# Linear attention's second product on whole 128x128 blocks instead of 64x64 and 128x64 pieces

## The chip, the cores and the metric

The kernel runs on one core of a Trainium2 chip. A core has a matrix engine (TensorE, PE in the profile; its weight loads are PEld), a vector engine (VectorE, DVE), a scalar engine (ScalarE, ACT), GpSimd (POOL) and SyncE (SP), which here issues the transfers. Each engine works through its own list of instructions in order; semaphores hold it until what it needs is there. The metric is the device time in microseconds (us) of one execution. Lower is better. Three runs of the kernel before gave 322.04, 321.97 and 322.44 us.

## The reference

One decoder layer on 256 tokens of width 1024, in fp32. An input projection feeds two groups of heads: MoBA, which is plain causal attention here, and GLA, a gated linear attention with 4 heads, keys of width 64 and values of width 128. Then come an output projection, a residual and a feed-forward part with a short convolution. The change is in GLA:

```python
def gla_attention(q, k, v, log_a):
    """S_t = diag(alpha_t) S_{t-1} + k_t^T v_t ;  o_t = q_t S_t."""
    ...
        decay = jnp.exp(jnp.where(causal[None, None, :, :, None], diff, -jnp.inf))
        A = jnp.einsum('bhtd,bhsd,bhtsd->bhts', q_, k_, decay)
        o = (jnp.einsum('bhts,bhsv->bhtv', A, v_)
             + jnp.einsum('bhtd,bhdv->bhtv', q_ * jnp.exp(G_), state))
```

Written without chunks, `o[t] = sum over s <= t of A[t, s] v[s]`, where `A[t, s]` is the product of query t and key s with the decay between them. `A` is causal: nothing stands where s is after t. Behind it, `o` is normed per head, multiplied by a gain and by the gate `silu(r)`.

## The kernel before

The 256 tokens are two token tiles of 128 (`tt` = 0, 1). Weights come in slots of 1 MB; ScalarE and VectorE split each into a high part `hi` (line 92) and a rest `lo` (line 95), and `mm3` multiplies in three products (lines 109 to 111). TensorE's list is in the order of the program text. The input projection and the first half of the output projection run in steps `q` = 0 to 55, and a table (`on(q, f, ...)`) says behind which step each piece of attention is put. The lists of ScalarE, VectorE, GpSimd and SyncE are ordered by the compiler's scheduler, except where the text fixes them (`g_tail`).

GLA first builds `A` transposed: rows are s, columns are t. There are 8 diagonal blocks of 128x128, one for each of 2 head pairs, 2 token tiles and 2 heads in a pair. A block has four quadrants of 64. The two on the diagonal, (s, t) both in the first half or both in the second, are collected in `ATd`: seven levels of halving (`lvl_a` to `lvl_d_`) write into it, on VectorE (line 376). The quadrant with s in the first half and t in the second comes from the level of 64, which `lvl_d_` copies from PSUM on ScalarE into rows 0 to 63 of `ATu` (line 371). `lvl_join` (line 379) copies the second diagonal quadrant below it, into rows 64 to 127 of `ATu`. The fourth quadrant, s in the second half and t in the first, is zero and is stored nowhere. `AT01` holds the blocks between the two token tiles, for the 4 heads (line 403).

`g_av(tt)` is the second product, `o = A v`, for one token tile, with the blocks as TensorE's stationary operand (weights) and the values `gv` as the moving one. For each head, with `o` a 128x128 part of one PSUM bank:

```python
if tt == 1:
    T.matmul(o, AT01[:, pr * 2 + hh], gv[:, 0, vs], start=True, stop=False)
i = (pr * 2 + tt) * 2 + hh
T.matmul(o[0:64], ATd[0:64, i], gv[0:64, tt, vs], start=(tt == 0), stop=True)
T.matmul(o[64:128], ATu[:, i], gv[:, tt, vs], start=(tt == 0), stop=True)
```

Lines 420 and 421 are the two pieces: tokens of the first half from 64 rows and 64 columns, tokens of the second half from 128 rows and 64 columns. Line 418 is a whole block. Both token tiles are put behind step 46, and two steps of the input projection and the last MoBA product (lines 526 and 527) stand between them and the output projection. Then `g_tail` norms both tiles on ScalarE and VectorE (lines 429, 177, 178, 435), loads the gate's table and evaluates the gate (line 409). `g_out` multiplies by the gate (line 450) and transposes (line 452), behind steps 53 and 54; its result is a part of the output projection's input.

Of the kernel before, what the change touches and what calls it, by code (L numbers as in the profile page):

```python
# [9 lines left out]
F32 = mybir.dt.float32  # L10
# [6 lines left out]
S = 256  # L17
KT = 8
# [9 lines left out]
LEVELS = [32, 16, 8, 4, 2, 1, 64]  # L28
# columns of the parameter array
P_FG, P_BG, P_CW, P_CB = 0, 8, 10, 10 + 3 * 2 * NP  # L30
# [4 lines left out]
def trunk_kernel(ctx: ExitStack, tc: tile.TileContext, xT_d, wG_d, w5_d, wo_d, up_d, dn_d,  # L35
# [16 lines left out]

    # ------------------------------------------------------------------ constants and parameters
    A.preload_act_table_set("natural_log_exp_and_others")
# [12 lines left out]

    # the tensor engine's clock rises while the first loads are under way
    warm = const.tile([128, 128], F32, name="warm")
# [4 lines left out]

    # ------------------------------------------------------------------ weights: load and split
    RAW, SPL = 4, 3
# [59 lines left out]

    # ------------------------------------------------------------------ x
    xg = main.tile([128, KT + KT * S], F32, name="xg")     # the first norm's gains, then x^T
    pag = xg[:, :KT]
# [33 lines left out]
    def rsqrt_t(r, ss, n, tmp):  # L173
        """r = (ss / n + EPS) ** -0.5 by logarithm and exponential, then a Newton step."""
        v, t = tmp
        V.tensor_scalar(v, ss, 1.0 / n, EPS, op0=ALU.mult, op1=ALU.add)
        A.activation(t, ss, AF.Ln, scale=1.0 / n, bias=eps)
        A.activation(r, t, AF.Exp, scale=-0.5)
        V.tensor_mul(t, r, r)
        V.scalar_tensor_tensor(t, t, -0.5, v, op0=ALU.mult, op1=ALU.mult)  # L180
        V.scalar_tensor_tensor(r, t, 1.5, r, op0=ALU.add, op1=ALU.mult)

    def rsqrt(r, ss, n, tmp):
        """r = (ss / n + EPS) ** -0.5: a seed from the exponent bits, then Newton steps. It yields
        between its steps, so that other work fits in."""
        v, t = tmp
        V.tensor_scalar(v, ss, 1.0 / n, EPS, op0=ALU.mult, op1=ALU.add)
        V.tensor_scalar(t.bitcast(I32), v.bitcast(I32), 1, None, op0=ALU.logical_shift_right)
        yield
        V.tensor_scalar(r.bitcast(I32), t.bitcast(I32), -1.0, float(0x5F3759DF),  # L190
                        op0=ALU.mult, op1=ALU.add)
        for _ in range(3):
            V.tensor_mul(t, r, r)
            yield
            V.scalar_tensor_tensor(t, t, -0.5, v, op0=ALU.mult, op1=ALU.mult)
            V.scalar_tensor_tensor(r, t, 1.5, r, op0=ALU.add, op1=ALU.mult)

    # ------------------------------------------------------------------ attention buffers
    ap_ = ctx.enter_context(ExitStack())
# [4 lines left out]
    Gc = at.tile([128, 512], F32, name="Gc")  # L204
    ATd = at.tile([128, 8, 64], F32, name="ATd")           # the blocks of 64 on the diagonal
    ATu = at.tile([128, 8, 64], F32, name="ATu")           # the second half's columns
    AT01 = at.tile([128, 4, 128], F32, name="AT01")
# [7 lines left out]
    for i in range(2):  # L215
        nc.gpsimd.memset(kts[i], 0.0)
        nc.gpsimd.memset(qts[i], 0.0)
    nc.gpsimd.memset(qt128, 0.0)
    mqT = at.tile([128, 4, S], F32, name="mqT")
    mkT = at.tile([128, 4, S], F32, name="mkT")  # L220
# [30 lines left out]
    def xrow():  # L251
        """The rotation's tables take up the norm, which lies along their rows here."""
        p = att()
        for tt in range(2):
            T.matmul(p[:, tt * 128:(tt + 1) * 128], rstd(tt).to_broadcast([128, 128]), ident,
                     start=True, stop=True)
        for t in (cos, sin):
            V.tensor_mul(t, t, p[:, :S])

    # ---- GLA  # L260
    def g_evac(tt):
# [19 lines left out]
    def g_diag():  # L281
        dgp = at.tile([128, 2, 256], F32, name="e", bufs=2)
        V.scalar_tensor_tensor(dgp, gqk[:, :, 0:256], DK ** -0.5, gqk[:, :, 272:528],
                               op0=ALU.mult, op1=ALU.mult)
        V.tensor_add(id64, ident[:, 0:64], ident[:, 64:128])
        dg = at.tile([128, 2, 2, 2], F32, name="dg")       # pair, ttile, head
        for tt in range(2):
            V.tensor_reduce(dg[:, :, tt, :], dgp[:, tt].rearrange("p (a h d) -> p a h d", a=2, h=2),
                            axis=mybir.AxisListType.X, op=ALU.add)
        for i in range(8):  # L290
            A.activation(ATd[:, i], id64, AF.Copy, scale=dg.rearrange("p a b c -> p (a b c)")[:, i:i + 1])
# [75 lines left out]
    def lvl_d_(l):  # L367
        b = LEVELS[l]
        p = st["lv", l]
        if b == 64:  # L370
            A.activation(ATu[0:64], p[0:64].rearrange("p (i t) -> p i t", i=8), AF.Copy)
            return
        n = 32 // b
        o = ATd.rearrange("p i (n two b) -> p i n two b", two=2, b=b)[:, :, :, 1, :]
        m = lvl[:, l].bitcast(I32).rearrange("p (n b) -> p n b", b=b)[:, None].to_broadcast([128, 8, n, b])
        V.copy_predicated(o, m, p[:, :256].rearrange("p (i n b) -> p i n b", i=8, b=b))  # L376

    def lvl_join():
        A.activation(ATu[64:128], ATd[64:128], AF.Copy)

# [30 lines left out]
    def g_av(tt):  # L411
        p = att()
        for h in range(HG):
            pr, hh = divmod(h, 2)
            o = p[:, h * DV:(h + 1) * DV]
            vs = slice(h * DV, (h + 1) * DV)
            if tt == 1:
                T.matmul(o, AT01[:, pr * 2 + hh], gv[:, 0, vs], start=True, stop=False)
            i = (pr * 2 + tt) * 2 + hh
            T.matmul(o[0:64], ATd[0:64, i], gv[0:64, tt, vs], start=(tt == 0), stop=True)  # L420
            T.matmul(o[64:128], ATu[:, i], gv[:, tt, vs], start=(tt == 0), stop=True)  # L421
        st["o", tt] = p
# [16 lines left out]
    def g_tail():  # L439
        # the norm's tables before the gate's: one change of tables  # L440
        with tc.manual_schedule(engines={mybir.EngineType.Activation}):
# [16 lines left out]

    # ---- MoBA (the sequence is one block, so a query's own block is all it attends to)
    def rope_a(which, n):  # L460
        """The halves of each head change places."""
        qs = at.tile([128, 512], F32, name="qs", bufs=2)
# [16 lines left out]
    def m_scores(pr):  # L479
        # two heads in turn, each in its half of the array's rows and in a bank of its own  # L480
        for hh in range(2):
# [50 lines left out]

    # ------------------------------------------------------------------ emission plan
    plan = {}
# [107 lines left out]

    # ------------------------------------------------------------------ output projection
    hh_ = main.tile([128, KT, S], F32R, name="hh", tag="ah")
# [33 lines left out]

    # ------------------------------------------------------------------ feed-forward
    downs = {}  # L680
# [91 lines left out]

    # the output's columns by bank; the last ones, which end the kernel, are fewer
    PIECES = (((0, 512), (512, 1024)), ((0, 512), (512, 768), (768, 1024)))
# [10 lines left out]
    def residual(tt, n):  # L785
        """The residual opens the down projection's sums."""
        a, b = PIECES[tt][n]
# [22 lines left out]

    # pair 0: its last contraction tile waits for the last columns of h
    up_alloc(0)
# [11 lines left out]
    lo(2, 1)  # L824
    # pair 1
    dload(1)
# [7 lines left out]
    for n, _ in enumerate(steps):  # L834
        if n < 4:
            ups[3].split_lo(512 * n, 512 * n + 512)
    # pair 2
    dload(2)
# [17 lines left out]
    gate_lo(0)  # L856
    # pair 3
    dload(3)
# [63 lines left out]
    A.preload_act_table_set("sqrt_and_others")  # L922
    # the last pair's gate is awaited behind one product of the second token tile
    for i in range(NP - 4, NP - 1):
# [10 lines left out]

    # ------------------------------------------------------------------ final norm
    fin = ff.tile([128, 24], F32, name="fin")
    yy = ff.tile([128, 2, D], F32, name="yy", tag="big")
    for tt in range(2):
# [4 lines left out]
        for n, (a, b) in enumerate(PIECES[tt]):  # L944
# [11 lines left out]
            if n < last:  # L956
                vb = v
                V.tensor_scalar(vh, v, -0.5, None, op0=ALU.mult)
        # r = (mean square + EPS) ** -0.5 with one Newton step
        A.activation(sq, ss, AF.Sqrt, scale=1.0 / D, bias=vb)  # L960
# [10 lines left out]
def _layout(inputs):  # L971
# [5 lines left out]
    def ktile(m):  # L977
        return m.reshape(-1, 128, m.shape[1]).transpose(1, 0, 2)      # [128, k, cols]

# [14 lines left out]
    fin_g = f(np.broadcast_to(a["final_norm_g"].reshape(1, D), (128, D)))  # L994
    # tables that depend on shapes alone
    inv = (1.0 / (np.float32(10000.0) ** (np.arange(0, HD, 2, dtype=np.float32) / np.float32(HD)))).astype(np.float32)
# [32 lines left out]
```

## Time and profile before

| | before |
|---|---|
| median of three runs | 322.04 us (321.97 to 322.44) |
| span of the profiled execution | 320.4 us |
| the time around that span, to the median | 1.6 us |
| mean granted TensorE clock | 0.994 |
| `g_av` in the profile | 92.46 to 99.90 us |
| products in `g_av` | 8 of 64 rows and 64 columns, 8 of 128 rows and 64 columns, 4 whole |

The profile is of one execution. Times in it count from the start of its span; the span leaves out about 1.6 us of what the runs' time includes. A row of the view in order of time gives start, duration, engine, line, operation, output<-inputs, size of the array used (rows*columns, for TensorE), shapes and count; behind it in brackets stands how long the engine was idle before, and what ended that. TensorE's rows overlap, since its products are pipelined, so that the distance of two starts says what an instruction takes of the stream. Every fp32 product is recorded twice (two passes, each with a weight load); the `hi`/`lo` products are recorded once.

### The profile page before, as it was taken

What the parts mean: (1) busy time and instruction counts of PE and PEld (TensorE: products, weight loads), DVE (VectorE), ACT (ScalarE), POOL (GpSimd) and SP (SyncE); (2) the same over time, 40 slices, a digit from 0 to 9 for tenths busy, and PEclk for the clock granted to TensorE, in tenths of its full rate; (3) what the DMA queues carried; (4) which work ended last, traced back from release to release, by engine and by line L of the source; (5) the groups of instructions that cost most, each with busy time, mean ns of one, the idle gap of its engine ahead of it and who ended that gap; (6) DMA issues with size and microseconds to landing.
All of it is one profiled execution on the core that took longest, in us unless ns stands there. A gap on an engine that the chain in (4) does not pass through costs nothing.

```text
span 320.4 us, 5873 instructions
## 1 busy us (share of the span) xinstructions
PE 312.3 (97%) x2312; PEld 285.9 (89%) x2312; DVE 253.7 (79%) x478; ACT 203.2 (63%) x369; POOL 3.5 (1%) x16
## 2 busy tenths in 40 slices
PE   8999999999999999999999999999999999999992
PEld 7999997776766999999999999999999999999982
DVE  3888999999634658899999987777787777776653
ACT  5978988588845748637677655555555555544353
POOL 4000000000000000000000000000000000000000
PEclk9999999999999999999999999999999999999997
DMA  6999433452360245379356555555555521110003
GB/s 186 387 415 402 183 133 131 139 186 79 125 262 1 103 163 190 140 282 370 127 212 254 202 196 196 199 196 198 197 196 199 218 111 68 65 67 1 2 0 132
DMA packets 12299, 55.39 MB, mean 173 GB/s; under 512 B 1376, under 2 KB 2928, under 8 KB 7920
## 3 DMA queue, kind: packets, MB, share of 16 engines
q1 hardware_dynamic: 12272, 55.02, 46.2%
q8 instruction: 18, 0.29, 0.4%
q14 instruction: 9, 0.07, 0.1%
HBM read 53.97 MB, written 1.05 MB: 172 GB/s over the span
## 4 chain that ended last, share of the span: by engine, by line
PE 79%; DVE 9%; ACT 5%; issue 2%; DMA 2%; SPq 1%; DVEq 0%; ACTq 0%
PE att L110 14%; PE att L109 14%; PE att L111 14%; PE acc L110 10%; PE acc L109 10%; PE acc L111 10%; DVE lo L95 2%; DMA xg<-in_xT 2%; ACT qs L465 1%; DVE qt L350 1%; DVE att L494 1%; PE att L421 1%; PE att L420 1%; PE att L526 1%; DVE ATd L376 1%
## 5 line engine op out<-in xcount | busy, mean ns | idle before, releaser
L92 ACT ACTIVATE hi<-raw 128x1024 fp32r<-128x1024 f32 (+3 forms) x84 | 80.1, 971 | 51.4 <-PE att L110 43.1
L95 DVE TENSOR_TENSOR lo<-raw,hi 128x1024 fp32r<-128x1024 f32 (+3 forms) x86 | 93.7, 1098 | 13.8 <-ACT hi L92 13.8
L109 PE MATMUL att<-hh,hi 128*128 128x256 f32 x352 | 98.6, 280 | 0.0
L111 PE MATMUL att<-hh,lo 128*128 128x256 f32 x352 | 98.4, 280 | 0.0
L110 PE MATMUL att<-hl,hi 128*128 128x256 f32 x352 | 98.4, 279 | 0.0
L109 PEld LDWEIGHTS att<-hh,hi 128*128 128x128 f32 x352 | 66.3, 188 | 0.0
L111 PEld LDWEIGHTS att<-hh,lo 128*128 128x128 f32 x352 | 66.2, 188 | 0.0
L110 PEld LDWEIGHTS att<-hl,hi 128*128 128x128 f32 x352 | 66.2, 188 | 0.0
L756 DVE SCALAR_TENSOR_TENSOR c<-us,par,c 128x256 f32<-128x256 f32 x88 | 40.7, 482 | 4.1 <-ACT c L748 2.5
L748 ACT ACTIVATE c<-us,par 128x256 f32<-128x256 f32 x44 | 24.0, 590 | 21.6 <-DVE us L738 16.1
L111 PE MATMUL acc<-dhi,gl 128*128 128x512 f32 (+1 forms) x88 | 32.3, 367 | 0.0
L110 PE MATMUL acc<-dlo,gh 128*128 128x512 f32 (+1 forms) x88 | 32.2, 366 | 0.0
L109 PE MATMUL acc<-dhi,gh 128*128 128x512 f32 (+1 forms) x88 | 31.8, 361 | 0.0
L695 DVE TENSOR_TENSOR dlo<-draw,dhi 128x1024 fp32r<-128x1024 f32 x22 | 26.7, 1220 | 0.0
L738 DVE TENSOR_TENSOR us<-att,rb 128x512 f32<-128x512 f32 x20 | 13.8, 690 | 15.9 <-PE att L111 15.9
L109 PE MATMUL acc<-hi,ah 128*128 128x512 f32 (+1 forms) x64 | 25.9, 404 | 0.2 <-ACT hi L92 0.2
L110 PE MATMUL acc<-lo,ah 128*128 128x512 f32 (+1 forms) x64 | 24.6, 384 | 0.4 <-DVE lo L95 0.4
L111 PE MATMUL acc<-hi,al 128*128 128x512 f32 (+1 forms) x64 | 24.1, 376 | 0.0
L690 ACT ACTIVATE dhi<-draw 128x1024 fp32r<-128x1024 f32 x22 | 23.1, 1048 | 0.0
L110 PEld LDWEIGHTS acc<-dlo,gh 128*128 128x128 f32 x88 | 16.5, 188 | 3.0
L109 PEld LDWEIGHTS acc<-dhi,gh 128*128 128x128 f32 x88 | 16.6, 188 | 2.9
L111 PEld LDWEIGHTS acc<-dhi,gl 128*128 128x128 f32 x88 | 16.5, 188 | 2.6
(192 smaller groups left out, 537.5 us busy)
## 6 DMA issues: line engine op xcount, KB each, us to landing
raw<-in_up SPq DMA_DIRECT2D x22, 1024.0 KB, 4.8
draw<-in_dn SPq DMA_DIRECT2D x22, 512.0 KB, 5.7
raw<-in_w SPq DMA_DIRECT2D x8, 1024.0 KB, 7.4
raw<-in_wo SPq DMA_DIRECT2D x4, 1024.0 KB, 4.7
raw<-in_w SPq DMA_DIRECT2D x4, 512.0 KB, 7.6
raw<-in_wG SPq DMA_DIRECT2D x2, 528.0 KB, 7.2
out_y<-yy SPq DMA_DIRECT2D x4, 256.0 KB, 2.2
raw<-in_wG SPq DMA_DIRECT2D x3, 264.0 KB, 4.8
```

The source lines that it names most:

```text
L92: A.activation(self.hi[:, a:b], self.raw[:, a:b], AF.Copy)
L95: V.tensor_sub(self.lo[:, a:b], self.raw[:, a:b], self.hi[:, a:b])
L109: T.matmul(out, sh, mh, start=first, stop=False, **kw)
L110: T.matmul(out, sh, ml, start=False, stop=False, **kw)
L111: T.matmul(out, sl, mh, start=False, stop=last, **kw)
L350: V.tensor_mul(o, q_, e_)
L376: V.copy_predicated(o, m, p[:, :256].rearrange("p (i n b) -> p i n b", i=8, b=b))
L690: A.activation(hi, downs[i][0], AF.Copy)
L695: V.tensor_sub(lo, d, hi)
L738: V.tensor_tensor(u[:, :, 2:], upo[i][2].rearrange("p (a t) -> p a t", a=2), rb[:, None, :].to_broadcast([128, 2, S]), op=ALU.mult)
L748: A.activation(cv[i][:, a], u[:, a, 2:], AF.Identity, bias=par[:, P_CB + m:P_CB + m + 1], scale=par[:, P_CW + 2 * 2 * NP + m:P_CW + 2 * 2 ...
L756: V.scalar_tensor_tensor(c[:, a], u[:, a, w:w + S], par[:, wc:wc + 1], c[:, a], op0=ALU.mult, op1=ALU.add)
```

## The change

The eight diagonal blocks are now kept whole, in one array `AT` (named `ATf` in the lists below) of 8 x 128 columns, which replaces `ATu`. Its zero quadrant is set once by GpSimd at the start. `lvl_d_` and `lvl_join` write the three other quadrants; `lvl_join` has one more copy. `g_av` multiplies each block in one product. `ATd` stays as it was, and is no longer read by TensorE. Comments were taken out as well, and lines behind 218 are one or two further on.

```diff
-    ATu = at.tile([128, 8, 64], F32, name="ATu")           # the second half's columns
+    AT = at.tile([128, 8, 128], F32, name="ATf")
...
     nc.gpsimd.memset(qt128, 0.0)
+    nc.gpsimd.memset(AT[64:128, :, 0:64], 0.0)
...
         if b == 64:
-            A.activation(ATu[0:64], p[0:64].rearrange("p (i t) -> p i t", i=8), AF.Copy)
+            A.activation(AT[0:64, :, 64:128], p[0:64].rearrange("p (i t) -> p i t", i=8), AF.Copy)
             return
...
     def lvl_join():
-        A.activation(ATu[64:128], ATd[64:128], AF.Copy)
+        A.activation(AT[64:128, :, 64:128], ATd[64:128], AF.Copy)
+        A.activation(AT[0:64, :, 0:64], ATd[0:64], AF.Copy)
...
             i = (pr * 2 + tt) * 2 + hh
-            T.matmul(o[0:64], ATd[0:64, i], gv[0:64, tt, vs], start=(tt == 0), stop=True)
-            T.matmul(o[64:128], ATu[:, i], gv[:, tt, vs], start=(tt == 0), stop=True)
+            T.matmul(o, AT[:, i], gv[:, tt, vs], start=(tt == 0), stop=True)
```

TensorE's list at `g_av`, from the last pieces of the first token tile on, before (`AT_126` is `AT01`):

```order
L420 MATMUL att<-gv,ATd 64x128
L421 MATMUL att<-gv,ATu 64x128
L418 MATMUL att<-gv,AT_126 128x128
L420 MATMUL att<-gv,ATd 64x128
L421 MATMUL att<-gv,ATu 64x128
```

and now, from the projection's product ahead of the first token tile (one row for its four blocks):

```order
L111 MATMUL acc<-hi,al 128x512
L422 MATMUL att<-gv,ATf 128x128 x4
L420 MATMUL att<-gv,AT_126 128x128
L422 MATMUL att<-gv,ATf 128x128
L420 MATMUL att<-gv,AT_126 128x128
```

The alternating pair of pieces has become one block per head, and no product of another size stands between the blocks. The rest of TensorE's list is in the same order as before.

ScalarE's list at the join, with what each row waits for, before (`pt` and `pe` are MoBA's softmax, `gv` the values):

```order
L516 ACTIVATE pt<-att 128x384 [waits PE_49]
L379 ACTIVATE ATu<-ATd 64x512 [waits DVE_49]
L506 ACTIVATE pe<-pe,mx 128x128 [waits DVE_49,Activation_49]
L406 ACTIVATE gv<-acc,rsx 128x512 [waits PE_49] x2
L499 ACTIVATE pe,mx<-att,mx 128x128 [waits DVE_49]
```

and now:

```order
L517 ACTIVATE pt<-att 128x384 [waits PE_49]
L380 ACTIVATE ATf<-ATd 64x8x64 [waits DVE_49]
L507 ACTIVATE pe<-pe,mx 128x128 [waits DVE_49,Activation_49]
L381 ACTIVATE ATf<-ATd 64x8x64
L408 ACTIVATE gv<-acc,rsx 128x512 [waits PE_49] x2
L500 ACTIVATE pe,mx<-att,mx 128x128 [waits DVE_49]
```

The second copy has come in between the softmax row and the copy of the values. Behind this place ScalarE's list is the same. VectorE's differs in one place (of the norm's four last rows, one instead of two stands ahead of the rest of the last MoBA pair), GpSimd's by the one memset, and SyncE's not at all.

## The prediction

> **What bounds the kernel now.** I read three views, in this order: the head of the page, the busy time by stage, and the instructions in order of time around the change.
>
> ```profile
> span 320.4 us, 5873 instructions
> PE 312.3 (97%) x2312; PEld 285.9 (89%) x2312; DVE 253.7 (79%) x478; ACT 203.2 (63%) x369; POOL 3.5 (1%) x16
> PE 79%; DVE 9%; ACT 5%; issue 2%; DMA 2%; SPq 1%; DVEq 0%; ACTq 0%
> ```
>
> TensorE is busy for 97% of the span and holds 79% of the chain that ended last. An average can hide a stage with another limit, so the stages come next; the columns are the stretch, its length, the busy time of PE, PEld, DVE, ACT and POOL, the granted clock, the DMA share and GB/s.
>
> ```profile
> 92.40:99.90 7.50, 7.50 (x41) 4.22 (x40) 1.78 (x8) 1.64 (x10) 0.00 (x0) 1.00 0.35 137
> 99.90:118.00 18.10, 18.10 (x143) 16.98 (x143) 9.92 (x19) 10.28 (x22) 0.22 (x3) 1.00 0.32 117
> 118.00:160.00 42.00, 42.00 (x354) 41.61 (x353) 39.45 (x72) 27.85 (x48) 0.00 (x0) 1.00 0.55 210
> 160.00:300.00 140.00, 140.00 (x1049) 133.35 (x1048) 114.15 (x174) 81.76 (x122) 0.00 (x0) 1.00 0.43 159
> 300.00:320.00 20.00, 14.64 (x91) 12.99 (x89) 10.51 (x31) 8.26 (x19) 0.00 (x0) 0.92 0.14 54
> ```
>
> The stretch 92.4 to 99.9 is the changed one (`g_av`). From its start to 300 us TensorE has no idle time at all, at a granted clock of 1.00. Time taken out of its stream there comes out of the end, as long as nothing else becomes late. In the stretch itself DVE and ACT work under a quarter of the time, so TensorE alone sets its length.
>
> **What the old products cost.** The next rows are TensorE's instructions in order of time: start, duration, line, output<-inputs, size of the array used, shape. An fp32 product is two records, each with its own weight load; I call a record a pass.
>
> ```profile
> 92.13 0.40 PE L111 MATMUL acc<-hi,al 128*128 128x512 f32 x1
> 92.46 0.43 PE L420 MATMUL att<-gv,ATd 64*64 64x128 f32 x2
> 92.82 0.43 PE L421 MATMUL att<-gv,ATu 128*64 128x128 f32 x2
> 95.34 0.49 PE L418 MATMUL att<-gv,AT 128*128 128x128 f32 x2
> 95.76 0.43 PE L420 MATMUL att<-gv,ATd 64*64 64x128 f32 x2
> ...
> 99.54 0.43 PE L421 MATMUL att<-gv,ATu 128*64 128x128 f32 x2
> 99.90 0.50 PE L109 MATMUL acc<-hi,ah 128*128 128x512 f32 x1
> 100.24 0.40 PE L110 MATMUL acc<-lo,ah 128*128 128x512 f32 x1
> ...
> 101.18 0.40 PE L111 MATMUL acc<-hi,al 128*128 128x512 f32 x1
> ```
>
> Durations overlap, so I go by starts. A 64-wide piece takes 0.36 us (92.46 to 92.82), whether 64 or 128 rows deep; the whole block L418 takes 0.42 us (95.34 to 95.76). The 16 pieces and 4 blocks make 16 x 0.36 + 4 x 0.42 = 7.44 us. With both edges it is a little more: from the L111 before (92.13) to the L110 behind (100.24) is 8.11 us; undisturbed, these two are two steps apart, and a step is (101.18 - 100.24) / 4 = 0.235 us. So `g_av` pushes the stream back by 8.11 - 0.47 = **7.64 us**.
>
> Why so dear? Three sizes of array alternate, and the weight loads do not run ahead:
>
> ```profile
> 92.81 0.19 PEld L421 LDWEIGHTS att<-gv,ATu 128*64 128x64 f32 x2 [0.17 <-issue]
> ```
>
> The load unit stands idle for 0.17 us ahead of each change of size, and nothing that the profile shows holds it. That is the reading on which the forecast rests: the switch costs, not the multiplying.
>
> **What the new products cost.** After the change there are 8 whole blocks of L422 and the 4 of L420 (the old L418), 24 passes, all 128*128 with 128 columns. The trace has this very form elsewhere, two products in a row in the same kind of stream (L715):
>
> ```profile
> 141.26 0.28 PE L109 MATMUL att<-hh,hi 128*128 128x256 f32 x1
> ...
> 141.49 0.28 PE L111 MATMUL att<-hh,lo 128*128 128x256 f32 x1
> 141.61 0.60 PE L715 MATMUL acc<-ident,rs 128*128 128x128 f32 x4
> 141.97 0.37 PE L109 MATMUL att<-hh,hi 128*128 128x256 f32 x1
> 142.18 0.28 PE L110 MATMUL att<-hl,hi 128*128 128x256 f32 x1
> ```
>
> Counted in the same way, edges included: from L111 (141.49) to L110 (142.18) is 0.69 us; two steps of this stream are 141.49 - 141.26 = 0.23 us; four passes cost 0.46 us, or 0.115 us each. A second row bounds it: L357, four 128*64 products in a row.
>
> ```profile
> 80.79 1.09 PE L357 MATMUL att<-qt,kt 128*64 128x128 f32 x8
> 81.72 0.65 PE L526 MATMUL att<-pt,mv 128*64 128x256 f32 x4
> ```
>
> 81.72 - 80.79 = 0.93 us for eight passes is 0.116 us each: 64-wide products are no dearer than whole ones where the size stays the same. 24 x 0.115 = **2.76 us**. The accumulation of L422 onto L420 in one bank is no new case, since the two passes of L715 also add up in one place.
>
> **The sum on TensorE**: 7.64 - 2.76 = 4.88 us less.
>
> Here a rule of the Trainium skill speaks on both sides: "TensorEngine Tiling (Array Packing)", section Key Properties, says that a change of tiling mode drains the engine, and that tiles of one mode can load and multiply in parallel. The first agrees with the 0.17 us of idle loads and gives the sum above. The second speaks against whole blocks; what it would make of the time is the second rival below.
>
> **What ScalarE and GpSimd get.** The join grows from one 64x512 copy to two, and its output gets gaps.
>
> ```profile
> 77.17 0.63 ACT L379 ACTIVATE ATu<-ATd 64x512 f32<-64x512 f32 x1
> 77.82 0.40 ACT L506 ACTIVATE pe<-pe,mx 128x128 f32<-128x128 f32 x1
> 78.48 1.38 ACT L406 ACTIVATE gv<-acc,rsx 128x512 f32<-128x512 f32 x2 [0.26 <-PE acc L111]
> 80.67 0.37 ACT L499 ACTIVATE pe<-att,mx 128x128 f32<-128x128 f32 x1 [0.81 <-DVE mx L496]
> ```
>
> One copy takes 0.65 us (77.17 to 77.82). The new one stands between L506 and L406. L406 would start 0.65 - 0.26 = 0.39 us later, and the 0.81 us of waiting for DVE behind it swallow that. Cost: nothing; the copied blocks are wanted 14 us later. The cost of a gapped output isn't in the trace; the ends are no extra cost, and twice the 0.65 us for both copies. Then L499 would start 3 x 0.65 - 0.26 - 0.81 = 0.9 us late, and TensorE's transposes behind it with it, if they have no room. I take the row as it is. The memset of the zero quadrant covers half the rows of the last one there:
>
> ```profile
> 3.24 0.52 POOL L218 MEMSET qt<- 128x512 f32 x1
> ```
>
> It ends near 4.3 us at the latest and is wanted at 92 us: nothing. Its cover is 88 us long. SyncE's order does not move.
>
> **What is late next?** Behind `g_av` ScalarE runs the norm, in order, and only then the copy of the last MoBA pair (L530), the gates and the splits of the weights.
>
> ```profile
> 95.45 0.28 ACT L429 ACTIVATE e<-att 128x128 f32<-128x128 f32 x1 [4.68 <-PE att L421]
> 100.01 0.28 ACT L429 ACTIVATE e<-att 128x128 f32<-128x128 f32 x1 [2.85 <-PE att L421]
> 101.51 0.20 ACT L178 ACTIVATE sm<-sm 128x4 f32<-128x4 f32 x1
> 102.44 0.39 ACT L530 ACTIVATE mh<-att 128x256 fp32r<-128x256 f32 x1 [0.72 <-PE att L527]
> ```
>
> The norm of a token tile takes 101.71 - 100.01 = 1.70 us of ScalarE. So far it lay beside the 4.6 us of the second tile's products. Now these are 16 passes, 16 x 0.115 = 1.84 us: still 0.14 us longer. The first tile ends near 92.13 + 0.235 + 8 x 0.115 = 93.3 us, the second near 95.1 us, and ScalarE is free for it within 0.1 us; L530 has 0.72 us of waiting to spare. The output transposes are the next that could wait:
>
> ```profile
> 104.86 0.69 DVE L450 TENSOR_TENSOR y<-y,gr 128x512 f32<-128x512 f32 x1 [0.98 <-ACT gr L409]
> 110.82 0.60 PE L452 MATMUL att<-ident,y 128*128 128x128 f32 x4
> ```
>
> Their input is there more than 5 us ahead, and both sides move together, since the gates follow L530 and L530 follows TensorE. From 118 us DVE is busy 39.45 of 42 us, but it enters that stage waiting for TensorE:
>
> ```profile
> 117.51 0.42 DVE L671 TENSOR_TENSOR xg<-acc,xg 128x256 f32<-128x256 f32 x1 [2.88 <-PE acc L111]
> ```
>
> So its work starts earlier by the same 4.9 us and is not squeezed. The loads are issued when DVE's splits free a slot; they move along. I charge nothing for all this.
>
> **Total.** Profiled span 320.4 - 4.9 = 315.5 us. The median of the runs, 322.04 us, is 1.6 us above that span; I keep this part and forecast 322.04 - 4.9 = **317.1 us**. With passes between 0.105 and 0.125 us (the rounding of the starts) and the spread of the runs it is 316.5 to 317.7 us.
>
> **Rivals.**
>
> *The blocks keep their old price.* L418 cost 0.42 us, not 0.23. Should that belong to the fp32 block with its weights freshly written, and not to the switch, 12 x 0.42 + 0.2 at the edges = 5.24 us, 2.4 us saved: 319.6 us. If only half of the 12 pay it, 6 x 0.42 + 6 x 0.23 + 0.2 = 4.1 us: 318.5 us. For it: it is the only price of these operands in the trace. Against it: L715 at 0.115 us a pass. Chance 0.10.
>
> *The halves had run side by side, and the zero quadrant throws that away.* Products of one size in the two column halves do overlap here:
>
> ```profile
> 101.50 0.66 PE L526 MATMUL att<-pt,mv 128*64 128x256 f32 x4
> 101.98 0.39 PE L527 MATMUL att<-pt,mv 128*64 128x128 f32 x4
> 102.31 0.50 PE L109 MATMUL acc<-hi,ah 128*128 128x512 f32 x1
> ```
>
> These passes stream 4 x 256 and 4 x 128 columns, 12 x 0.115 = 1.38 us in a row, and took 0.81 us. If L420 and L421 shared their 0.36 us slots in this way, a whole block would cost both, 0.72 us, and the time would stay at 322.0 us. Against it: a piece's 0.36 us for two passes of 128 columns is more than the 0.23 us that L357 needs for two without any partner, so nothing is shared there. This is what the skill's rule of parallel tiles ("TensorEngine Tiling (Array Packing)", Key Properties) would give; here the sizes differ, which its rule of the drain covers. Chance 0.04, and 0.03 more for the gain being waited away at a place that I called covered (317.7 to 322).
>
> *Slower: the clock.* If the denser weight stream made the granted clock fall in the 205 us from 95 to 300 us, each 0.01 would cost 2.1 us; the gain is gone at 0.977, and at 0.96 the time is 317.1 + 205 x (1 / 0.96 - 1) = 325.6 us. Against it: 1.00 in every stage to 300 us, though these streams have no gaps either, and the new piece lasts 3 us. Chance 0.02.
>
> **How the numbers follow.** Forecast 0.81; old price 0.10; halves 0.04; waited away 0.03; clock 0.02. The range 316.5 to 318.6 us holds the forecast and the old price paid by up to half of the blocks, about 0.86 less what I may have mis-sized at the lower end. A measurement here tells 0.2% (0.64 us) from no change. Faster by more: 0.81 + 0.10 + 0.02 = 0.93; within: 0.05; slower: 0.02.
>
> **What would show it.** In the trace after: from the last L111 before the blocks to the second product behind them 3.2 us instead of 8.11; no 0.17 us of idle loads between the blocks; 2296 TensorE records instead of 2312; TensorE busy near 307.4 us; the transposes of L452 at about 106 us instead of 110.82; all stages to the end as long as before. A step of 0.42 us between blocks shows the first rival. Idle time of TensorE before 105 us shows a cover that was gone: before 92 us the copies, behind it the norm.

## The result, and the profile after

| | before | after |
|---|---|---|
| median | 322.01 us (4 runs, 321.97 to 322.44) | 317.06 us (4 runs, 317.00 to 317.25) |
| after / before | | 0.9845, 95% interval 0.9831 to 0.9859 |
| span of the profiled execution | 320.4 us | 315.4 us |
| `g_av`, from the last product ahead to the second behind, less two steps | 7.64 us | 2.67 us |
| records on TensorE | 2312 | 2296 |

The forecast was 317.1 us. The head of the page after:

```profile
span 315.4 us, 5842 instructions
PE 305.8 (97%) x2296; PEld 282.5 (90%) x2296; DVE 253.5 (80%) x478; ACT 203.7 (65%) x370; POOL 3.9 (1%) x17
PE 79%; DVE 10%; ACT 5%; issue 2%; DMA 2%; SPq 1%; DVEq 0%; ACTq 0%
```

The bound has not changed: TensorE, with the same shares of the span and of the chain. TensorE in order of time at the changed place (start, duration, line, output<-inputs, size of the array, shape, count):

```profile
91.91 0.40 PE L111 MATMUL acc<-hi,al 128*128 128x512 f32 x1
92.15 1.05 PE L422 MATMUL att<-gv,ATf 128*128 128x128 f32 x8
93.04 0.39 PE L420 MATMUL att<-gv,AT 128*128 128x128 f32 x2
93.26 0.39 PE L422 MATMUL att<-gv,ATf 128*128 128x128 f32 x2
...
94.60 0.39 PE L422 MATMUL att<-gv,ATf 128*128 128x128 f32 x2
94.74 0.47 PE L109 MATMUL acc<-hi,ah 128*128 128x512 f32 x1
95.05 0.39 PE L110 MATMUL acc<-lo,ah 128*128 128x512 f32 x1
```

From L111 (91.91) to L110 (95.05) is 3.14 us; less two steps, 0.47 us, this is 2.67 us, or 0.111 us for each of the 24 passes. The loads run ahead of their products now (91.91 ahead of 92.15, 92.93 ahead of 93.04), and nothing stands in brackets behind them:

```profile
91.91 1.09 PEld L422 LDWEIGHTS att<-gv,ATf 128*128 128x128 f32 x8
92.93 0.30 PEld L420 LDWEIGHTS att<-gv,AT 128*128 128x128 f32 x2
```

`g_av` gave 7.64 - 2.67 = 4.97 us, and the medians differ by 4.95 us: all of it reached the end. By stage (columns as in the prediction, each stage moved by 4.8 to 4.9 us):

```profile
95.10:113.10 18.00, 18.00 (x145) 16.92 (x144) 11.64 (x26) 10.51 (x22) 0.17 (x3) 1.00 0.34 122
113.10:155.10 42.00, 42.00 (x355) 41.61 (x354) 39.45 (x72) 27.86 (x49) 0.00 (x0) 1.00 0.57 212
155.10:295.10 140.00, 140.00 (x1050) 133.34 (x1049) 113.81 (x174) 81.49 (x121) 0.00 (x0) 1.00 0.44 159
```

TensorE has no idle time from the change to 295 us, at a clock of 1.00, and a stage holds the same number of records but one or two (145 for 143 in a stage that is 0.1 us shorter here, 355 for 354, 1050 for 1049). The feed-forward stages are the old ones, 5 us earlier.

What was called covered, on ScalarE, VectorE and TensorE:

```profile
76.96 0.63 ACT L380 ACTIVATE ATf<-ATd 64x512 f32<-64x512 f32 x1
77.60 0.40 ACT L507 ACTIVATE pe<-pe,mx 128x128 f32<-128x128 f32 x1
77.91 0.62 ACT L381 ACTIVATE ATf<-ATd 64x512 f32<-64x512 f32 x1
78.43 1.25 ACT L408 ACTIVATE gv<-acc,rsx 128x512 f32<-128x512 f32 x2
80.44 0.37 ACT L500 ACTIVATE pe<-att,mx 128x128 f32<-128x128 f32 x1 [0.76 <-DVE mx L497]
...
97.25 0.39 ACT L531 ACTIVATE mh<-att 128x256 fp32r<-128x256 f32 x1 [0.51 <-PE att L528]
```

```profile
112.33 0.43 DVE L672 TENSOR_TENSOR xg<-acc,xg 128x256 f32<-128x256 f32 x1 [2.88 <-PE acc L111]
105.63 0.60 PE L453 MATMUL att<-ident,y 128*128 128x128 f32 x4
```

Behind the new copy (L381, 0.62 us) 0.76 us of waiting for VectorE are left, of 0.81 us. The last MoBA copy (L531) still waits for TensorE, 0.51 us. VectorE still enters the next stage with 2.88 us of waiting, to the hundredth what it was. The transposes stand at 105.63 instead of 110.82.

### The profile page after: what moved, and what is told of

Read it like the earlier page. It is cut to its first block, busy times and chain, and to the rows that moved or that the text cites. A ratio compares the mean times of both kernels' runs of the same rounds, so it can differ in the third digit from the quotient of the medians.

```text
span 315.4 us, 5842 instructions
## 1 busy us (share of the span) xinstructions
PE 305.8 (97%) x2296; PEld 282.5 (90%) x2296; DVE 253.5 (80%) x478; ACT 203.7 (65%) x370; POOL 3.9 (1%) x17
## 4 chain that ended last, share of the span: by engine, by line
PE 79%; DVE 10%; ACT 5%; issue 2%; DMA 2%; SPq 1%; DVEq 0%; ACTq 0%
PE att L110 14%; PE att L111 14%; PE att L109 14%; PE acc L110 11%; PE acc L109 10%; PE acc L111 10%; DVE lo L95 2%; DMA xg<-in_xT 2%; ACT qs L466 1%; DVE qt L351 1%; DVE att L495 1%; PE att L527 1%; DVE ATd L377 1%; DVE kt L345 1%; PE att L515 1%
## 5 line engine op out<-in xcount | busy, mean ns | idle before, releaser
L111 PE MATMUL att<-hh,lo 128*128 128x256 f32 x352 | 98.4, 279 | 0.0
L110 PE MATMUL att<-hl,hi 128*128 128x256 f32 x352 | 98.3, 279 | 0.0
L111 PEld LDWEIGHTS att<-hh,lo 128*128 128x128 f32 x352 | 66.2, 188 | 0.0
L110 PEld LDWEIGHTS att<-hl,hi 128*128 128x128 f32 x352 | 66.2, 188 | 0.0
L111 PE MATMUL acc<-dhi,gl 128*128 128x512 f32 (+1 forms) x88 | 32.3, 367 | 0.0
L110 PE MATMUL acc<-dlo,gh 128*128 128x512 f32 (+1 forms) x88 | 32.2, 366 | 0.0
L109 PE MATMUL acc<-hi,ah 128*128 128x512 f32 (+1 forms) x64 | 25.2, 394 | 1.2 <-ACT hi L92 1.2
L110 PE MATMUL acc<-lo,ah 128*128 128x512 f32 (+1 forms) x64 | 24.1, 376 | 0.8 <-DVE lo L95 0.8
L111 PE MATMUL acc<-hi,al 128*128 128x512 f32 (+1 forms) x64 | 23.6, 368 | 0.0
L691 ACT ACTIVATE dhi<-draw 128x1024 fp32r<-128x1024 f32 x22 | 23.1, 1049 | 0.0
L110 PEld LDWEIGHTS acc<-dlo,gh 128*128 128x128 f32 x88 | 16.5, 188 | 3.0
L111 PEld LDWEIGHTS acc<-dhi,gl 128*128 128x128 f32 x88 | 16.5, 188 | 2.6
```

The lines of the kernel that those rows point to most:

```text
L109: T.matmul(out, sh, mh, start=first, stop=False, **kw)
L110: T.matmul(out, sh, ml, start=False, stop=False, **kw)
L111: T.matmul(out, sl, mh, start=False, stop=last, **kw)
L691: A.activation(hi, downs[i][0], AF.Copy)
```

## The experiments

The theory: TensorE's stream sets the time one to one. In it a pass of 128 columns costs 0.111 us, and each change of the size of the array costs about 0.15 us more; the 64-wide pieces are not dear in themselves. The rivals: dear pieces; the number of products; some of the gain from the new array or the copies; a cost of the copies that the gain hides. All kernels ran against the kernel before on the same chip. "`g_av`" is again the time from the last product ahead to the second behind, less two steps.

**The array and the copies without the new products.** In the changed kernel:

```diff
-            T.matmul(o, AT[:, i], gv[:, tt, vs], start=(tt == 0), stop=True)
+            T.matmul(o[0:64], AT[0:64, i, 0:64], gv[0:64, tt, vs], start=(tt == 0), stop=True)
+            T.matmul(o[64:128], AT[:, i, 64:128], gv[:, tt, vs], start=(tt == 0), stop=True)
```

> The changed kernel with the old products: the whole array, its memset and its extra copy stay, but g_av reads it in the old 64x64 and 128x64 pieces. My theory (only TensorE's stream counts, the copies are covered): 7.6 us from the last product ahead to the second behind, net of two steps, as before, and a time of 322.0 us. Rival (the new array or the moved copies give part of the gain): below 321.4 us. Rival (the copies cost something that the gain hid): above 322.6 us.

Measured: 322.12 us, ratio 1.0002 (0.9993 to 1.0012). TensorE's rows at both edges:

```profile
91.53 0.40 PE L111 MATMUL acc<-hi,al 128*128 128x512 f32 x1
91.86 0.43 PE L422 MATMUL att<-gv,ATf 64*64 64x128 f32 x2
92.22 0.43 PE L423 MATMUL att<-gv,ATf 128*64 128x128 f32 x2
...
99.64 0.40 PE L110 MATMUL acc<-lo,ah 128*128 128x512 f32 x1
```

99.64 - 91.53 - 0.47 = 7.64 us, as before. The array, the memset and the copies neither give nor cost anything that can be measured (the interval leaves room for 0.2 us less to 0.4 us more). The gain is in the products. Nor is it the change from one array of weights to another that costs: here both pieces come from `ATf` at the old price, and in the changed kernel `ATf` and `AT01` alternate without one.

**The same products in another order.** In the kernel before; `start` is set at the first head of a bank only, and `stop` at its last:

```diff
-        for h in range(HG):
...
+        for h0 in range(0, HG, 4):
+            hs = [(h, h // 2, h % 2, p[:, h * DV:(h + 1) * DV], slice(h * DV, (h + 1) * DV))
+                  for h in range(h0, h0 + 4)]
             if tt == 1:
-                T.matmul(o, AT01[:, pr * 2 + hh], gv[:, 0, vs], start=True, stop=False)
...
+                for h, pr, hh, o, vs in hs:
+                    T.matmul(o, AT01[:, pr * 2 + hh], gv[:, 0, vs], start=(h == 0), stop=False,
+                             skip_group_check=True)
+            for h, pr, hh, o, vs in hs:
+                i = (pr * 2 + tt) * 2 + hh
+                T.matmul(o[0:64], ATd[0:64, i], gv[0:64, tt, vs], start=(tt == 0 and h == 0), stop=(h == HG - 1),
+                         skip_group_check=True)
+            for h, pr, hh, o, vs in hs:
+                i = (pr * 2 + tt) * 2 + hh
+                T.matmul(o[64:128], ATu[:, i], gv[:, tt, vs], start=(tt == 0 and h == 0), stop=(h == HG - 1),
+                         skip_group_check=True)
```

> The kernel before with the same 20 products in another order: for each token tile the 4 whole blocks, then the 4 pieces of 64x64, then the 4 of 128x64. The size of the array changes 6 times instead of 21. Theory of the switch: 40 passes at 0.111 us are 4.45 us, and the other 3.2 us of the 7.64 are 21 changes at 0.15 us; so 4.45 + 6 x 0.15 = 5.4 us in g_av, and a time of 319.7 us. Rival (64-wide pieces are dear in themselves, 0.36 us each): 322.0 us. Rival (the number of products counts, not their order): 322.0 us.

Measured: 319.77 us, ratio 0.9922 (0.9906 to 0.9939). TensorE, then its loads:

```profile
92.00 0.40 PE L111 MATMUL acc<-hi,al 128*128 128x512 f32 x1
92.32 1.08 PE L422 MATMUL att<-gv,ATd 64*64 64x128 f32 x8
93.34 1.09 PE L426 MATMUL att<-gv,ATu 128*64 128x128 f32 x8
94.36 1.16 PE L418 MATMUL att<-gv,AT 128*128 128x128 f32 x8
95.44 1.08 PE L422 MATMUL att<-gv,ATd 64*64 64x128 f32 x8
96.46 1.09 PE L426 MATMUL att<-gv,ATu 128*64 128x128 f32 x8
97.47 0.50 PE L109 MATMUL acc<-hi,ah 128*128 128x512 f32 x1
97.81 0.40 PE L110 MATMUL acc<-lo,ah 128*128 128x512 f32 x1
```

```profile
92.32 0.84 PEld L422 LDWEIGHTS att<-gv,ATd 64*64 64x64 f32 x8 [0.37 <-issue]
93.33 0.85 PEld L426 LDWEIGHTS att<-gv,ATu 128*64 128x64 f32 x8 [0.17 <-issue]
94.35 0.97 PEld L418 LDWEIGHTS att<-gv,AT 128*128 128x128 f32 x8 [0.17 <-issue]
```

97.81 - 92.00 - 0.47 = 5.34 us for the same 20 products. Eight passes of a narrow size take 1.02 us, and a whole size's eight take 1.08 us: 8 x 0.111 = 0.89 us and 0.13 or 0.19 us for the change that ends them. The idle time of the loads stands at the changes, and the view shows none inside a group: 0.37 us ahead of the first, 0.17 us ahead of a change from a narrow size, and 0.12 us behind the whole blocks (the next load starts at 95.44), which the view doesn't print. Dear pieces and the number of products both fall: neither was touched.

**The same in groups of two heads.** Against the edit above:

```diff
-        for h0 in range(0, HG, 4):
+        for h0 in range(0, HG, 2):
...
-                  for h in range(h0, h0 + 4)]
+                  for h in range(h0, h0 + 2)]
```

> As the grouped order, but in groups of two heads: 11 changes of size, the same 20 products. Theory of the switch: 4.45 + 11 x 0.15 = 6.1 us in g_av, and 320.5 us. Rivals as there: 322.0 us.

Measured: 320.58 us, ratio 0.9948 (0.9933 to 0.9963). `g_av` in its trace:

```profile
91.95 0.40 PE L111 MATMUL acc<-hi,al 128*128 128x512 f32 x1
...
94.02 0.65 PE L426 MATMUL att<-gv,ATu 128*64 128x128 f32 x4
94.60 0.71 PE L418 MATMUL att<-gv,AT 128*128 128x128 f32 x4
95.24 0.65 PE L422 MATMUL att<-gv,ATd 64*64 64x128 f32 x4
...
98.54 0.39 PE L110 MATMUL acc<-lo,ah 128*128 128x512 f32 x1
```

6.59 - 0.47 = 6.12 us. Against the order before, 10 changes fewer gave 1.52 us, and the next 5 gave 0.78 us: 0.152 and 0.156 us a change, a straight line. `start` and `stop` are set in the same way in both grouped kernels, so they don't make the difference between these two. The rows also give both prices without any borrowed number. Groups of two, four and eight narrow passes take 0.36, 0.58 and 1.02 us up to the next start: 0.11 us a pass and 0.14 us for the change. The whole blocks of `AT01` take 0.42, 0.64 and 1.08 us: again 0.11 us a pass, and 0.20 us for the change.

**Halves of one size.** In the changed kernel:

```diff
-            if tt == 1:
-                T.matmul(o, AT01[:, pr * 2 + hh], gv[:, 0, vs], start=True, stop=False)
             i = (pr * 2 + tt) * 2 + hh
-            T.matmul(o, AT[:, i], gv[:, tt, vs], start=(tt == 0), stop=True)
+            for c in (0, 64):
+                if tt == 1:
+                    T.matmul(o[c:c + 64], AT01[:, pr * 2 + hh, c:c + 64], gv[:, 0, vs], start=True, stop=False)
+            for c in (0, 64):
+                T.matmul(o[c:c + 64], AT[:, i, c:c + 64], gv[:, tt, vs], start=(tt == 0), stop=True)
```

> The changed kernel with every block cut in two halves of 64 columns, the blocks between the token tiles too: 24 products of 128x64 and no other size, halves in turn; 48 passes, 2 changes of size. Theory of the switch, if the halves run side by side as in the last MoBA product (0.81 us for what takes 1.38 us in a row): 48 x 0.0655 + 2 x 0.15 = 3.4 us and 317.9 us. Without any overlap: 48 x 0.111 + 0.3 = 5.6 us and 320.0 us. Rival (64-wide pieces cost 0.36 us each whatever stands beside them): 24 x 0.36 = 8.6 us and 323.0 us.

Measured: 317.41 us, ratio 0.9847 (0.9829 to 0.9865).

```profile
91.89 0.40 PE L111 MATMUL acc<-hi,al 128*128 128x512 f32 x1
92.21 1.09 PE L424 MATMUL att<-gv,ATf 128*64 128x128 f32 x16
93.14 0.39 PE L422 MATMUL att<-gv,AT 128*64 128x128 f32 x4
...
95.32 0.39 PE L110 MATMUL acc<-lo,ah 128*128 128x512 f32 x1
```

Sixteen passes take 0.93 us (92.21 to 93.14), 0.058 us each: the two halves run side by side, fully; the MoBA product had let me expect 0.0655 us. A change of size stands behind that product; without 0.15 us for it, its 0.81 us come to 0.055 us for each of 12 passes of 128 columns (an estimate). `g_av` is 95.32 - 91.89 - 0.47 = 2.96 us, the 2.67 of the whole blocks and 0.29 us for two changes of size. So a whole block is no better than its halves; it is better than halves of *different* sizes. The products write rows 0 to 63 and 64 to 127 of the bank in turn, as the old pieces did, so that isn't what cost. The times of this kernel and the changed one can't be told apart; the traces can.

**The changed kernel again**, beside the next two:

> The changed kernel again, beside the two that follow: 317.1 us.

Measured: 317.08 us, ratio 0.9844 (0.9829 to 0.9859).

**More copies.** In the changed kernel:

```diff
         A.activation(AT[0:64, :, 0:64], ATd[0:64], AF.Copy)
+        A.activation(AT[0:64, :, 0:64], ATd[0:64], AF.Copy)
+        A.activation(AT[0:64, :, 0:64], ATd[0:64], AF.Copy)
```

> The changed kernel with the join's new copy made three times. ScalarE stood idle for 0.76 us behind the copy of the values; two more copies at 0.62 us fill this and put 0.5 us on what follows. Theory (the copy costs nothing while that idle time lasts): 317.1 us if TensorE's transposes behind it have 0.5 us of room, 317.6 us at most. Rival (each copy costs its own length): 317.1 + 1.2 = 318.3 us.

Measured: 317.62 us, ratio 0.9861 (0.9846 to 0.9875). That is 0.54 us over the run above; the intervals overlap, but all four times of this kernel (317.56 to 317.80) lie above all four there (316.88 to 317.44). Its trace shows a part of it:

```profile
80.28 1.09 PE L358 MATMUL att<-qt,kt 128*64 128x128 f32 x8
81.46 0.66 PE L529 MATMUL att<-pt,mv 128*64 128x256 f32 x4
```

From L358 to the MoBA product behind it are 1.18 us, where the run above has 0.92 us (80.80 to 81.72): 0.26 us for 1.2 us of copies. TensorE waits there for a copy of the softmax (`pt`) that ScalarE now makes later. From the last product ahead of `g_av` to ScalarE's last instruction both traces take 219.19 us, so where the other 0.28 us of the medians went is not shown. The copy of the change itself is covered; another two are not quite.

**Eight blocks twice.** In the changed kernel, the four blocks of the first token tile and the four of `AT01` are multiplied two times, the first time with a result that is thrown away.

```diff
-                T.matmul(o, AT01[:, pr * 2 + hh], gv[:, 0, vs], start=True, stop=False)
...
+                for stop in (True, False):
+                    T.matmul(o, AT01[:, pr * 2 + hh], gv[:, 0, vs], start=True, stop=stop)
+            else:
+                T.matmul(o, AT[:, i], gv[:, tt, vs], start=True, stop=True)
```

> The changed kernel with 8 of its 12 whole products made twice: 16 more passes of the one size. Theory (a pass is 0.111 us, and TensorE's stream goes into the time one to one): 1.8 us more, 318.9 us. Rival (whole blocks of these operands are dear, and the gain came from elsewhere): 8 x 0.42 = 3.4 us more, 320.4 us. Rival (something behind g_av now sets the pace): under 0.9 us more, below 318.0 us.

Measured: 319.06 us, ratio 0.9903 (0.9886 to 0.9919), 2.0 us over the run of the changed kernel beside it.

```profile
92.06 0.40 PE L111 MATMUL acc<-hi,al 128*128 128x512 f32 x1
...
96.99 0.39 PE L110 MATMUL acc<-lo,ah 128*128 128x512 f32 x1
```

`g_av` is 4.93 - 0.47 = 4.46 us, 1.79 us more for 16 passes, 0.112 us each. This is also the missing point of the line: 40 passes, as before, without a change of size (all of whole blocks, but a narrow pass costs the same 0.11 us). All together:

| kernel | passes | changes of size | `g_av` | time |
|---|---|---|---|---|
| before | 40 | 21 | 7.64 us | 322.0 us |
| groups of two heads | 40 | 11 | 6.12 us | 320.6 us |
| groups of four | 40 | 6 | 5.34 us | 319.8 us |
| eight blocks twice | 40 | 0 | 4.46 us | 319.1 us |
| after | 24 | 0 | 2.67 us | 317.1 us |

## Why the prediction was right

- **The bound.** TensorE's stream has no idle time from `g_av` to 300 us (295 us after), and the time moved with `g_av` in all five kernels of the table (2.2 us of time for the 2.30 us between the first and the third row, 2.0 for the 1.79 between the last two).
- **The old price**, 7.64 us, was read right, and its reason holds. The runs split it: 4.46 us for 40 passes and 3.18 us for 21 changes of size. The prediction's "the switch costs, not the multiplying" was a little strong: of the 4.97 us gained, 3.18 us are the changes and 1.79 us the 16 passes that went.
- **The new price** was 2.67 us for a forecast 2.76 us. L715 was the right row; 0.111 for 0.115 us a pass lies within the rounding of starts that are 0.69 us apart.
- **The copies and the norm** were covered, though not by the prediction's sum. It took 0.39 us off the wait behind the copies, which should have left 0.42 us; 0.76 us are left. In ScalarE's list the new copy takes 0.52 us from start to start (77.91 to 78.43) where 0.65 us were put, and the two copies of the values behind it took 1.25 us instead of 1.38. The gapped output, whose price might have doubled, costs nothing: 0.63 and 0.62 us, as the one without gaps (0.63 us). The last MoBA copy still waits for TensorE, 0.51 us.
- **The rivals.** The old price of L418 was its change of size: four more of its passes cost 0.44 us in the groups of four against the groups of two, 0.22 us a product. The prediction has 0.17 us of idle loads ahead of each change; behind a whole block it is 0.12 us, which changes nothing in the sum. The halves do run side by side when they have one size; the old pieces, 64x64 beside 128x64, did not, so that the zero quadrant throws nothing away against the old form. The rule on parallel tiles in the Trainium skill ("TensorEngine Tiling (Array Packing)", Key Properties) is true in the run of halves, at 0.058 us a pass, and its rule that a change of mode drains the engine agrees with the price of a change, about 0.15 us here; that the drain is what takes this time is not shown apart from that. The clock stayed at 1.00 to 295 us.
- **What missed:** TensorE's busy time fell by 6.5 us, to 305.8, where 307.4 was forecast. Of the 1.5 us beyond `g_av` 1.35 us lie in the start:

```profile
4.00:8.00 4.00, 3.73 (x14) 3.16 (x15) 2.48 (x6) 2.43 (x6) 0.00 (x0) 1.00 0.90 245
```

```profile
4.00:8.00 4.00, 2.38 (x13) 1.77 (x13) 2.33 (x6) 2.54 (x6) 0.35 (x1) 1.00 0.87 244
```

The first row is of before, the second of after: the same stretch, 14 and 13 records, 1.35 us less busy. Nothing was won by it: the product of the next weights starts at 7.35 us before and at 7.33 us after. Before, slower products fill the time up to it; after, TensorE waits 0.86 us for ScalarE's split of those weights. The change doesn't set this: the run of halves, with the new array and its memset, has 3.70 us in that stretch, and the run of the old products in the new array 2.57 us.

## What to carry to other kernels

Read the size of the array in TensorE's rows, not only the amount of work: where sizes alternate and the loads stand idle ahead of each change, every change has a price of its own (0.15 us here, more than a pass of 128 columns), and padding a piece with zeros up to its neighbour's size was cheaper than the change: a pair of pieces took 0.72 us, the whole block in its place 0.22 us. If padding isn't possible, sort the products by size: the same instructions in another order gave back 2.3 of the 5 us. And count on such a gain in full only where the stream has no idle time from there to the end.

## What the runs showed of the hardware that was not expected

- Halves of 128 rows and 64 columns, in turn and in one bank, run fully side by side: 0.058 us a pass, where the whole blocks take 0.111 us for twice the columns.
- The products of the first microseconds can take quite different times in two executions, at a granted clock of 1.00 in the records of both (3.73 and 2.38 us busy for 14 and 13 of them); what sets it is open.
- The place of `g_av` in the span differs by up to 0.6 us between the traces, ahead of any changed product (its last product ahead starts at 91.53 to 92.14 us; at 91.91 and 92.14 us in the two of the changed kernel). Two kernels are therefore better compared by the distance between two rows than by the start of one.
